# Two decoder layers on one Trainium2 core: loads, the memory branch and the merge's input reordered, a pair's copies ahead of its rests, four tiles normalised on VectorE alone

## The chip, the core and the metric

The kernel runs on one core of one Trainium2 chip. The metric is the device time of one execution in microseconds (us), the median of a few runs; lower is better.

## The reference, cut to what matters

Two layers run over x of 1024 tokens by 1024 features. Each layer projects x once, runs four attention branches of four heads each, weights them with learned gates, multiplies by an output matrix and normalises.

```python
def _layer(x, mem, ...):
    h = x @ w_in
    (c_q, c_kv, k_rope, sb_qkv, fox_qkv, fox_f, mem_q, gate_z, merge_r) = _split_last(h, IN_SPLITS)
    q  = _rms_norm(c_q, q_norm) @ w_qb          # MLA: low-rank queries, keys and values
    kv = _rms_norm(c_kv, kv_norm) @ w_kvb
    y_mla = _causal_softmax_attention(q with rope, k with rope, v_mla)
    y_sb  = _stick_breaking_attention(sq, sk, sv)
    y_fox = _causal_softmax_attention(fq, fk, fv, log_decay=c)
    mk, mv = jnp.split(mem @ w_mem_kv, 2, axis=-1)
    y_mem = _memory_attention(mem_q, mk, mv)    # mem: 256 rows
    merge_g = sigmoid(merge_r @ w_merge_up)
    merged = sum over n of merge_g[n] * ((branches[n] * silu(gate_z[n])) @ w_branch[n])
    return _layer_norm(ALPHA * x + merged @ w_out, ln_g, ln_b)
```

## The kernel before

All matrix products run on TensorE in a float32 form that rounds its operands. To keep float32 accuracy each operand is kept as two tiles, a rounded copy ("h") and the rest ("l" = value minus copy), and each product is three matmuls, h by h, l by h, h by l (`passes`, lines 233 to 239, seen in the trace as L236 to L238). The copy is made by ScalarE out of PSUM and the rest by VectorE from the same PSUM tile and the copy (`split_evac`, L145 and L146, with a scale L148 and L149). A pair of heads is stacked in the 128 rows of one product; `stack_pair` (L282, L283) makes the copy and the rest of rows 0 to 63 in tile opA and of rows 64 to 127 in opB. `v_from_T` (L300, L301), `mla_v` (L903, L904) and the memory keys (L778, L779) do the same for their operands. Weights come in as a stream of 128x512 tiles (`wload`: DMA on SP's queue into "wr", three buffers), and GpSimd splits each (`split_pool`, L154 and L157) into wh and wl, four buffers each.

A layer goes like this. Transposed x (`xT`, 8 column blocks by 2 halves of 512 tokens, each as h and l) stays in SBUF. First come the `pA` products (8 token blocks, lines 619 to 630). Then the branches: fox pair 0 and 1, stick-breaking ("sb") pair 0 and 1, memory ("mem"), MLA. `run` interleaves the attention of one pair with the projections of the next. Before the memory branch, `mem_prep` (757 to 787) loads the 1 MB of transposed mem, splits it, and projects memory keys and values with 8 weight tiles; `cq_norm` (744 to 752) sums squares with eight one-column products; the query projection of memory pair 0 follows. Then `last_gates` projects the last gates; between its halves the input of the merge is split (`split_mr`, `split_y`, lines 1076 to 1078) and the weights `wq` are loaded; then `main` (1085) interleaves the MLA input (`mla_ckvT`, `mla_k`, `mla_v`, ...) with the rest of the gates and the first merge steps. `merge` forms gate times branch product. At a layer's end the output product `po` runs over 8 token tiles twice (left and right 512 columns); after the right one `ln(t)` normalises tile t. Tiles 0 to 5 go VectorE (statistics), ScalarE (L1160), GpSimd (gain, L1161), VectorE (bias, L1163). Tiles 6 and 7, marked `direct`, take four VectorE instructions instead (L1149, L1155). In the first layer `transpose_x` (201 to 209) makes xT of the next layer's first half, woven into the products of tiles 6 and 7.

Instructions stand in each engine's queue in an order that is fixed at compile time. A planner (`schedule_with_timeline_sim=True`) writes it from the program order as priority and from its own estimate of durations; the engines then execute in that order, each waiting where an operand or buffer isn't ready. `after(later, earlier)` adds an edge that only orders two instructions. SBUF tiles of 128x512 float32 come from one pool of 64 ("U").

Of the kernel before, what the change touches and what calls it, by code (L numbers as in the profile page):

```python
# [65 lines left out]
def decoder_trunk(ctx: ExitStack, tc: tile.TileContext, x, x_t, mem_t, positions, w_a, w_s, mla_q_norm, mla_w_qb,  # L66
# [223 lines left out]
    def v_from_T(vT, nblk):  # L290
        v = []
        for b0 in range(0, nblk, 4):
# [4 lines left out]
            for b in range(0, n, 2):  # L297
                t = U("v").rearrange("p (b h c) -> p b h c", b=2, h=2)
                s = ps[:, b * P:(b + 2) * P].rearrange("p (b h c) -> p b h c", b=2, h=2)
                act.copy(t[:, :, :, 0:64], s)  # L300
                dve.tensor_tensor(t[:, :, :, 64:128], s, f(t[:, :, :, 0:64]), ALU.subtract)  # L301
# [274 lines left out]
    nc.sync.dma_start(pos_i, positions.rearrange("o (b p) -> p (o b)", p=P), allow_slow_non_contiguous=True)  # L576
# [29 lines left out]
    for layer in range(DEPTH):  # L606
# [32 lines left out]
        nc.sync.dma_start(fb, fox_forget_bias[layer].partition_broadcast(P))  # L639
# [76 lines left out]
        def evac_mr(ps, half):  # L716
            mr[half] = U("mr", F32)
            act.copy(mr[half], ps)
# [4 lines left out]
        nc.sync.dma_start(gq, mla_q_norm[layer].rearrange("(k p) -> p k", p=P), allow_slow_non_contiguous=True)  # L723
        nc.sync.dma_start(gk, mla_kv_norm[layer].rearrange("(k p) -> p k", p=P), allow_slow_non_contiguous=True)
# [32 lines left out]
        def mem_prep():  # L757
            memT = []
            raws = []
            for k0 in range(0, KT, 2):  # L760
                raw = U("memr", F32).rearrange("p (k c) -> p k c", k=2)
                nc.sync.dma_start(raw, mem_t[k0 * P:(k0 + 2) * P, :].rearrange("(k p) c -> p k c", p=P))
                raws.append(raw)
            for raw in raws:
# [4 lines left out]
            yield  # L769
            for pair in range(2):  # L770
# [5 lines left out]
                for t, r0 in zip(ks, (0, 64)):  # L776
                    lo = 64 - r0
                    act.copy(t[r0:r0 + 64, :], ps[r0:r0 + 64, :MEM])  # L778
# [48 lines left out]
        drain(weave(mem_prep(), cq_norm(), 4))  # L827
        drain(proj(stack_pair(mo[0]["q"], SC64)))
# [63 lines left out]
        def mla_v(half):  # L892
            for b in range(0, 4, 2):
# [108 lines left out]
        def split_y(n, half):  # L1002
            for pair in range(2):
# [6 lines left out]

        def split_mr():
            for half in range(2):
                h, l = U("mrh"), U("mrl")
                split_evac(mr[half], h, l)
                mr[half] = (h, l)
# [251 lines left out]
```

## Time and profile before

| | us |
|---|---|
| median of 3 runs (1605.41 to 1606.14) | 1605.91 |
| the profiled execution | 1603.06 |
| its span, first to last instruction | 1601.3 |
| TensorE (PE) busy | 1562.6 (98%) |
| VectorE (DVE) busy | 1040.0 (65%) |
| GpSimd (POOL) busy | 807.4 (50%) |
| ScalarE (ACT) busy | 740.5 (46%) |
| mean granted TensorE clock | 0.996 of full |

PE is the matmul stream, PEld its weight loads; matmuls overlap, so each is listed longer than the distance to the next. SPq is the queue of DMA issues. An instruction's row in a timeline ends with the idle time of its engine just before it and what ended that time.

### The profile page before, as it was taken

How to read it: one execution, taken by the hardware profiler on the slowest of the kernel's cores; microseconds unless marked ns; L12 is line 12 of the kernel's file. 1: busy time of each engine (PE TensorE's matmuls, PEld its weight loads, DVE VectorE, ACT ScalarE, POOL GpSimd, SP SyncE). 2: the span in 40 equal slices, each digit the busy share in tenths (PEclk: the TensorE clock that was granted, in tenths of full speed). 3: DMA queues.
4: the chain of work that ended last, by engine and by line, in shares of the span. 5: the costliest groups of instructions: out<-in, count | busy, mean ns of one | idle time of the engine just before them, and what ended most of it. 6: DMA issues, size and time to landing. Idle time of an engine off the chain costs nothing. (4 is left out here: it accounts for less than half of the span.)

```text
span 1601.3 us, 24815 instructions
## 1 busy us (share of the span) xinstructions
PE 1562.6 (98%) x8454; PEld 1330.3 (83%) x8454; DVE 1040.0 (65%) x2051; ACT 740.5 (46%) x1632; POOL 807.4 (50%) x967
## 2 busy tenths in 40 slices
PE   9999999999999999999999999999999999999997
PEld 7888888888878788888898888888888778888885
DVE  6365689834436788872763566997344367888737
ACT  4355565534425666440323556565344356564302
POOL 5675535755563233671426665357655623446503
PEclk9999999999999999999999999999999999999998
DMA  5321112142233211252312221122322322212413
GB/s 182 110 60 54 47 43 64 50 119 62 78 121 92 70 37 60 79 172 79 115 61 86 63 59 42 37 71 79 92 60 83 120 83 70 64 43 80 145 53 112
DMA packets 86062, 127.93 MB, mean 80 GB/s; under 512 B 13424, under 2 KB 38832, under 8 KB 85936
## 3 DMA queue, kind: packets, MB, share of 16 engines
q1 hardware_dynamic: 85936, 126.34, 25.5%
q8 instruction: 67, 1.10, 0.3%
q14 instruction: 59, 0.48, 0.1%
HBM read 89.57 MB, written 19.96 MB: 68 GB/s over the span
## 5 line engine op out<-in xcount | busy, mean ns | idle before, releaser
L236 PE MATMUL pj<-xTh,wh 128*128 128x512 f32 x832 | 329.9, 397 | 2.4 <-DVE mx L400 1.4
L238 PE MATMUL pj<-xTh,wl 128*128 128x512 f32 x832 | 326.2, 393 | 0.0
L237 PE MATMUL pj<-xTl,wh 128*128 128x512 f32 x832 | 325.8, 392 | 0.0
L157 POOL TENSOR_TENSOR wl<-wr,wh 128x512 fp32r<-128x512 f32 x168 | 225.7, 1345 | 9.0
L146 DVE TENSOR_TENSOR pl<-pt,ph 128x384 fp32r<-128x384 f32 (+1 forms) x272 | 170.6, 639 | 70.8 <-ACT ph L145 68.1
L154 POOL TENSOR_SCALAR wh<-wr 128x512 fp32r<-128x512 f32 x168 | 115.9, 690 | 198.2 <-PE pj L237 101.1
L145 ACT CAST ph<-pt 128x384 fp32r<-128x384 f32 (+1 forms) x272 | 146.4, 551 | 131.9 <-PE pt L431 128.0
L412 POOL TENSOR_SCALAR p<-p,sm 128x896 f32<-128x896 f32 (+7 forms) x128 | 102.2, 799 | 167.1 <-DVE sm L411 165.1
L238 PEld LDWEIGHTS pj<-xTh,wl 128*128 128x128 f32 x832 | 156.2, 188 | 32.1
L236 PEld LDWEIGHTS pj<-xTh,wh 128*128 128x128 f32 x832 | 156.6, 188 | 29.3 <-DVE mx L400 1.8
L237 PEld LDWEIGHTS pj<-xTl,wh 128*128 128x128 f32 x832 | 156.5, 188 | 26.1
L125 ACT ACTIVATE p<-p,mx 128x896 f32<-128x896 f32 (+7 forms) x128 | 99.5, 777 | 67.1 <-DVE mx L400 60.4
L461 PE MATMUL y<-pl,v 128*128 128x256 f32 (+1 forms) x544 | 121.4, 303 | 0.0
L461 PE MATMUL y<-ph,v 128*128 128x256 f32 (+1 forms) x544 | 111.4, 283 | 1.7 <-ACT ph L145 1.6
L125 ACT ACTIVATE mg<-pg 128x512 f32<-128x512 f32 x128 | 76.4, 597 | 75.0 <-PE pg L238 46.7
L431 PE MATMUL pt<-ident_r,p 128*128 128x128 f32 x704 | 110.7, 273 | 0.0
L236 PE MATMUL pb<-ybh,wh 128*128 128x512 f32 x256 | 103.0, 402 | 3.5 <-ACT mg L125 2.1
L461 PEld LDWEIGHTS y<-ph,v 128*128 128x128 f32 x544 | 93.1, 189 | 14.9 <-ACT ph L145 2.9
L405 DVE TENSOR_TENSOR_SCAN kt<-kt,unseen 128x896 f32<-128x896 f32 (+3 forms) x64 | 97.9, 1542 | 10.0 <-ACT kt L125 9.8
L392 POOL TENSOR_SCALAR_AFFINE_SELECT bt<-bt 128x128 f32<-128x128 f32 x64 | 52.9, 831 | 94.2 <-ACT bt L125 85.3
L237 PE MATMUL pb<-ybl,wh 128*128 128x512 f32 x256 | 100.2, 391 | 0.0
L238 PE MATMUL pb<-ybh,wl 128*128 128x512 f32 x256 | 100.1, 391 | 0.0
(275 smaller groups left out, 3634.6 us busy)
## 6 DMA issues: line engine op xcount, KB each, us to landing
wr<-in_w_s_dram SPq DMA_DIRECT2D x168, 256.0 KB, 2.6
s<-opA SPq DMA_DIRECT2D x128, 64.0 KB, 2.0
s<-opB SPq DMA_DIRECT2D x128, 64.0 KB, 2.0
wr<-in_w_out_dram SPq DMA_DIRECT2D x32, 256.0 KB, 2.7
xr<-in_x_t_dram SPq DMA_DIRECT2D x16, 256.0 KB, 5.7
ckb<-c_d SPq DMA_DIRECT2D x8, 512.0 KB, 3.8
y_d<-y SPq DMA_DIRECT2D x16, 256.0 KB, 2.0
y<-y_d SPq DMA_DIRECT2D x16, 256.0 KB, 3.3
```

Of the source, the lines that this page charges most:

```text
L125: i = act.activation(*args, **kw)
L145: act.copy(h, src)
L146: return dve.tensor_tensor(l, src, f(h), ALU.subtract)
L154: i = pool.tensor_scalar(h, src, 1.0, 1.0, ALU.mult, ALU.mult)
L157: pool.tensor_tensor(l, src, f(h), ALU.subtract)
L236: pe.matmul(ps, ah, bh, start=k == 0, stop=False)
L237: pe.matmul(ps, ah, bl, start=False, stop=False)
L238: pe.matmul(ps, al, bh, start=False, stop=k == nk - 1)
L405: dve.tensor_tensor_scan(kt[:, ::-1], kt[:, ::-1], unseen[:, S - w:][:, ::-1], 1.0, ALU.mult, ALU.max)
L412: pool.tensor_scalar(p, p, sm, 1.0, ALU.mult, ALU.mult)
L431: pe.transpose(pt[:, c:c + P], self.p[i][:, b * P:(b + 1) * P], ident)
L461: pe.matmul(u.y[:, q0 * P:256], u.op["v"][b][:, u.head, :], src[:, s * 256 + q0 * P:s * 256 + 256], start=j == 0 and n == 0, stop=j == n_c ...
```

## The change

Eight edits:

1. The first four weight loads, the positions, the forget bias and the two norm gains are ordered behind the last load of x on SP's queue.
2. `stack_pair`, `v_from_T`, the memory keys and `mla_v` issue both copies of a pair first and then both rests.
3. `merge_r` is split as soon as its product is done (`evac_mr`); `split_mr` goes.
4. Memory: the loads are issued, then the query projection of memory pair 0 runs with the split of mem and `cq_norm` (now in nine steps and more) woven in one step per pass, and the key and value projections come after. The weight stream is reordered to match.
5. The split of the fox branch for the merge is cut in four steps inside `main`, behind `mla_k(0)` and `mla_k(1)`; the load of wq goes to the same place.
6. `ln` takes the direct form from tile 4 on.
7. `transpose_x` of the first half starts after tile 4 and not 5.
8. Its splits take VectorE out: ScalarE copies PSUM to a raw tile, ScalarE copies again for h, GpSimd forms l.

```diff
-    def transpose_x(half, tiles):
+    def transpose_x(half, tiles, apart=False):
...
-            split_evac(ps, h, l)
+            if apart:
+                raw = U("xTr", F32)
+                act.copy(raw, ps)
+                act.copy(h, raw)
+                pool.tensor_tensor(l, raw, f(h), ALU.subtract)
+            else:
+                split_evac(ps, h, l)
...
-        nc.sync.dma_start(raw, w_s[n])
+        i = nc.sync.dma_start(raw, w_s[n])
+        if n < 4:
+            after(i, last_load[0])
...
             for t, r0 in ((a, 0), (b, 64)):
+                act.activation(t[r0:r0 + 64, :], ps[r0:r0 + 64, :], AF.Copy, scale=scale)
+            for t, r0 in ((a, 0), (b, 64)):
                 lo = 64 - r0
-                act.activation(t[r0:r0 + 64, :], ps[r0:r0 + 64, :], AF.Copy, scale=scale)
                 dve.scalar_tensor_tensor(t[lo:lo + 64, :], ps[r0:r0 + 64, :], scale, f(t[r0:r0 + 64, :]),
                                          ALU.mult, ALU.subtract)
...
-        nc.sync.dma_start(raw, x_t[k * P:(k + 1) * P, half * HALF:(half + 1) * HALF])
+        last_load[0] = nc.sync.dma_start(raw, x_t[k * P:(k + 1) * P, half * HALF:(half + 1) * HALF])
...
         def evac_mr(ps, half):
-            mr[half] = U("mr", F32)
-            act.copy(mr[half], ps)
+            h, l = U("mrh"), U("mrl")
+            split_evac(ps, h, l)
+            mr[half] = (h, l)
...
                 pe.matmul(ps[:, 2 * b:2 * b + 1], sq[b // 4][:, (b % 4) * P:(b % 4) * P + P], ones[:, 0:1], start=True, stop=True)
+                yield
...
-        drain(weave(mem_prep(), cq_norm(), 4))
-        drain(proj(stack_pair(mo[0]["q"], SC64)))
+        load_mem()
+        drain(weave(proj(stack_pair(mo[0]["q"], SC64)), chain(split_mem(), cq_norm()), 1))
+        drain(mem_prep())
...
-        split_mr()
-        split_y(2, 0)
-        split_y(2, 1)
-        load_wq()
...
-        main = chain(mla_ckvT(), mla_k(0), mla_k(1), step(lambda: load_cq(1)), mla_v(0), mla_v(1),
+        def split_2(half, pair):
+            return step(lambda: split_y(2, half, [pair]))
+
+        main = chain(mla_ckvT(), mla_k(0), split_2(0, 0), mla_k(1), split_2(0, 1), step(load_wq), step(lambda: load_cq(1)),
+                     split_2(1, 0), split_2(1, 1), mla_v(0), mla_v(1),
...
-            direct = t >= NB - 2
+            direct = t >= 4
...
+                    if t == 4 and not last_layer:
+                        early_x = transpose_x(0, [nat.pop(i) for i in range(4)], True)
                     if t == 5 and not last_layer:
-                        early_x = transpose_x(0, [nat.pop(i) for i in range(4)])
...
+    res += tile_of(w_in, MQ0)
     for c0 in (0, 256, P, 256 + P):
         res += tile_of(w_mem, c0)
-    for pair in range(2):
-        res += tile_of(w_in, MQ0 + pair * P)
+    res += tile_of(w_in, MQ0 + P)
```

## Rows read from the trace of the kernel before

**Rows 1.** The page: the span, and the busy time of each engine with its share of the span and its instructions.

```profile
span 1601.3 us, 24815 instructions
PE 1562.6 (98%) x8454; PEld 1330.3 (83%) x8454; DVE 1040.0 (65%) x2051; ACT 740.5 (46%) x1632; POOL 807.4 (50%) x967
```

**Rows 2.** Stretches of 20 us: stretch, length, busy time (and instructions) of PE, PEld, DVE, ACT and POOL, then the granted clock, the DMA share and GB/s. The first lies in stick-breaking attention of layer 1, the others at the merge's input of layers 1 and 2.

```profile
280.00:300.00 20.00, 18.80 (x106) 15.70 (x106) 18.16 (x19) 9.57 (x22) 15.81 (x14) 1.00 0.19 60
460.00:480.00 20.00, 17.59 (x82) 14.17 (x80) 9.27 (x11) 6.25 (x11) 14.18 (x19) 0.91 0.30 94
1260.00:1280.00 20.00, 17.59 (x90) 14.30 (x90) 11.81 (x15) 9.58 (x17) 16.20 (x21) 1.00 0.31 93
```

**Rows 3.** What PE waited for in the whole span: waiting line, releaser, us in total, times, longest.

```profile
PE pb L236 <- ACT mg L125: 2.1, 3, 0.9
PE mk L237 <- DVE meml L146: 1.1, 4, 0.3
PE pA L238 <- DVE xTl L146: 1.1, 2, 0.9
PE pg L236 <- DVE opB L283: 0.9, 2, 0.5
PE mk L236 <- ACT memh L145: 0.5, 2, 0.3
```

**Rows 4.** The start, timeline of SP's queue and of PE: start, length, engine, line, operation, count. The second SP row is the loads of x's second half; the PE row is the first product that reads a streamed weight tile.

```profile
10.92 1.48 SPq L214 DMA_DIRECT2D wr<-in_w_s_dram  x2
14.44 3.87 SPq L530 DMA_DIRECT2D xr<-in_x_t_dram  x8
...
35.04 0.39 PE L236 MATMUL pj<-xTh,wh 128*128 128x512 f32 x1
```

**Rows 5.** The merge's input: VectorE's timeline in layer 1; PE's timeline from the end of its wait to the next product of the gates, layer 1 and then layer 2; and a stretch of 2 us in layer 1, with the granted clock behind POOL's busy time.

```profile
465.98 2.40 DVE L146 TENSOR_TENSOR mrl<-mr,mrh 128x512 fp32r<-128x512 f32 x2
468.30 3.51 DVE L149 SCALAR_TENSOR_TENSOR ybl<-y,ybh 128x512 fp32r<-128x512 f32 x4
...
472.54 0.73 PE L866 MATMUL ckT<-ident_r,ckv 128*128 128x128 f32 x4 [2.41 <-DVE ckTl L149]
476.45 0.40 PE L236 MATMUL pj<-xTh,wh 128*128 128x512 f32 x1
1268.80 0.66 PE L866 MATMUL ckT<-ident_r,ckv 128*128 128x128 f32 x4 [2.41 <-DVE ckTl L149]
1271.13 0.39 PE L236 MATMUL pj<-xTh,wh 128*128 128x512 f32 x1
...
474.00:476.00 2.00, 2.00 (x8) 1.65 (x7) 0.75 (x1) 0.56 (x1) 1.71 (x4) 0.50 0.67 190
```

**Rows 6.** A pair's copies and rests: ScalarE's wait for VectorE over the whole span; then timelines of VectorE, ScalarE and PE at `mla_k` in layer 1.

```profile
ACT opB L282 <- DVE opA L283: 33.2, 37, 3.6
...
482.32 0.68 DVE L283 SCALAR_TENSOR_TENSOR opA<-pj,opA 64x512 fp32r<-64x512 f32 x1 [5.41 <-ACT opA L282]
483.04 0.59 ACT L282 ACTIVATE opB<-pj 64x512 fp32r<-64x512 f32 x1 [0.75 <-DVE opA L283]
488.58 0.69 DVE L283 SCALAR_TENSOR_TENSOR opB<-pj,opB 64x512 fp32r<-64x512 f32 x1 [0.72 <-ACT opB L282]
490.65 0.69 DVE L283 SCALAR_TENSOR_TENSOR opB<-pj,opB 64x512 fp32r<-64x512 f32 x1 [0.66 <-ACT opB L282]
489.42 0.47 PE L236 MATMUL pg<-mrh,wh 128*128 128x512 f32 x1 [0.46 <-DVE opB L283]
491.29 0.50 PE L236 MATMUL pb<-ybh,wh 128*128 128x512 f32 x1 [0.94 <-ACT mg L125]
```

**Rows 7.** The memory branch: GpSimd's two instructions for a weight tile (groups of the page: count, busy us, mean ns), and two matmuls of PE's timeline with 14 others of the same kind between them.

```profile
L157 POOL TENSOR_TENSOR wl<-wr,wh 128x512 fp32r<-128x512 f32 x168 | 225.7, 1345 | 9.0
L154 POOL TENSOR_SCALAR wh<-wr 128x512 fp32r<-128x512 f32 x168 | 115.9, 690 | 198.2 <-PE pj L237 101.1
...
330.40 0.28 PE L236 MATMUL mv<-memh,wh 128*128 128x256 f32 x1
332.20 0.28 PE L236 MATMUL mk<-memh,wh 128*128 128x256 f32 x1
```

**Rows 8.** The boundary between the layers: VectorE's and PE's timelines.

```profile
792.11 2.99 DVE L1163 TENSOR_TENSOR xo<-xo,lnp 128x512 f32<-128x512 f32 x2 [2.31 <-POOL xo L1161]
801.23 0.40 PE L236 MATMUL pA<-wAh,xTh 128*128 128x292 f32 x1 [1.16 <-DVE xTl L146]
808.05 0.40 PE L237 MATMUL pA<-wAl,xTh 128*128 128x292 f32 x1 [0.39 <-POOL wAl L553]
```

**Rows 9.** The end of layer 2: VectorE's timeline (L1193 takes the product of a tile: tile 4, 5 and 7 here; L1163 at 1587.67 is tile 5's; the last row is the last work of the kernel but for its store), and PE's last matmul.

```profile
1573.77 0.69 DVE L1193 SCALAR_TENSOR_TENSOR res<-xr,po 128x512 f32<-128x512 f32 x1 [0.28 <-DMA out_dram<-xo]
1579.21 0.69 DVE L1193 SCALAR_TENSOR_TENSOR res<-xr,po 128x512 f32<-128x512 f32 x1
1587.67 1.76 DVE L1163 TENSOR_TENSOR xo<-xo,lnp 128x512 f32<-128x512 f32 x1 [0.74 <-POOL xo L1161]
1593.30 0.68 DVE L1193 SCALAR_TENSOR_TENSOR res<-xr,po 128x512 f32<-128x512 f32 x1
1597.01 1.41 DVE L1155 SCALAR_TENSOR_TENSOR xo<-xo,rstd,lnp 128x512 f32<-128x512 f32 x2
...
1589.66 0.39 PE L238 MATMUL po<-woh,mgl 128*128 128x512 f32 x1
```

More of the change, by code (lines that the diff above doesn't have):

```diff
@@ L296, in v_from_T @@
                 pe.transpose(ps[:, b * P:(b + 1) * P], vT[b0 // 4][:, b * P:(b + 1) * P], ident)
-            for b in range(0, n, 2):
-                t = U("v").rearrange("p (b h c) -> p b h c", b=2, h=2)
-                s = ps[:, b * P:(b + 2) * P].rearrange("p (b h c) -> p b h c", b=2, h=2)
+            ts = [(U("v").rearrange("p (b h c) -> p b h c", b=2, h=2),
+                   ps[:, b * P:(b + 2) * P].rearrange("p (b h c) -> p b h c", b=2, h=2)) for b in range(0, n, 2)]
+            for t, s in ts:
                 act.copy(t[:, :, :, 0:64], s)
+            for t, s in ts:
                 dve.tensor_tensor(t[:, :, :, 64:128], s, f(t[:, :, :, 0:64]), ALU.subtract)
@@ L575, in decoder_trunk @@
     pos_i = cp.tile([P, NB], I32, name="pos_i")
-    nc.sync.dma_start(pos_i, positions.rearrange("o (b p) -> p (o b)", p=P), allow_slow_non_contiguous=True)
+    after(nc.sync.dma_start(pos_i, positions.rearrange("o (b p) -> p (o b)", p=P), allow_slow_non_contiguous=True), last_load[0])
     pos_f = cp.tile([P, NB], F32, name="pos_f")
@@ L638, in decoder_trunk @@
         fb = tp.tile([P, 4], F32, tag="fb", name=nm("fb"), bufs=1)
-        nc.sync.dma_start(fb, fox_forget_bias[layer].partition_broadcast(P))
+        after(nc.sync.dma_start(fb, fox_forget_bias[layer].partition_broadcast(P)), last_load[0])
         for h in range(4):
@@ L716, in evac_mr @@
         def evac_mr(ps, half):
-            mr[half] = U("mr", F32)
-            act.copy(mr[half], ps)
+            h, l = U("mrh"), U("mrl")
+            split_evac(ps, h, l)
+            mr[half] = (h, l)
         gq = tp.tile([P, 3], F32, tag="gq", name=nm("gq"), bufs=1)
         gk = tp.tile([P, 2], F32, tag="gk", name=nm("gk"), bufs=1)
-        nc.sync.dma_start(gq, mla_q_norm[layer].rearrange("(k p) -> p k", p=P), allow_slow_non_contiguous=True)
-        nc.sync.dma_start(gk, mla_kv_norm[layer].rearrange("(k p) -> p k", p=P), allow_slow_non_contiguous=True)
+        for g, src in ((gq, mla_q_norm), (gk, mla_kv_norm)):
+            after(nc.sync.dma_start(g, src[layer].rearrange("(k p) -> p k", p=P), allow_slow_non_contiguous=True), last_load[0])
         sq = [None, None]
@@ L755, in decoder_trunk, with load_mem @@
         mo = [{}, {}]
[L757 to L759 removed]
+        memT = []
+        mem_raws = []
+        def load_mem():
             for k0 in range(0, KT, 2):
@@ L762, in mem_prep, with split_mem @@
                 nc.sync.dma_start(raw, mem_t[k0 * P:(k0 + 2) * P, :].rearrange("(k p) c -> p k c", p=P))
-                raws.append(raw)
-            for raw in raws:
+                mem_raws.append(raw)
+        def split_mem():
+            for raw in mem_raws:
                 h, l = U("memh"), U("meml")
@@ L776, in mem_prep @@
                 for t, r0 in zip(ks, (0, 64)):
+                    act.copy(t[r0:r0 + 64, :], ps[r0:r0 + 64, :MEM])
+                for t, r0 in zip(ks, (0, 64)):
                     lo = 64 - r0
-                    act.copy(t[r0:r0 + 64, :], ps[r0:r0 + 64, :MEM])
                     dve.tensor_tensor(t[lo:lo + 64, :], ps[r0:r0 + 64, :MEM], f(t[r0:r0 + 64, :]), ALU.subtract)
@@ L899, in mla_v @@
                                       [(wkv_h[k][:, 256:], wkv_l[k][:, 256:]) for k in range(2)], 2)
-                for i in range(2):
-                    t = U("v").rearrange("p (h c) -> p h c", h=4)
-                    src = ps[:, i * 256:(i + 1) * 256].rearrange("p (h c) -> p h c", h=4)
+                ts = [(U("v").rearrange("p (h c) -> p h c", h=4),
+                       ps[:, i * 256:(i + 1) * 256].rearrange("p (h c) -> p h c", h=4)) for i in range(2)]
+                for t, src in ts:
                     act.copy(t[:, :, 0:64], src)
+                for t, src in ts:
                     dve.tensor_tensor(t[:, :, 64:128], src, f(t[:, :, 0:64]), ALU.subtract)
@@ L1000, in load_y, with split_y @@
                         nc.sync.dma_start(y, y_d[r:r + P, half * HALF:(half + 1) * HALF])
-        def split_y(n, half):
-            for pair in range(2):
+        def split_y(n, half, pairs=range(2)):
+            for pair in pairs:
                 h, l = U("ybh"), U("ybl")
@@ L1009, in decoder_trunk @@
         merged = {}
[L1011 to L1015, printed above, removed]
         def merge(n, first, final, following, also=None):
```

6 lines of the change are left out of this document (4 added, 2 removed).

## The prediction

> **What bounds the kernel now.** I read the page first: of a span of 1601.3 us TensorE is busy 1562.6 us, 98% [rows 1]. No other engine is above 65%. So the kernel is TensorE's stream of matmuls plus 38.7 us in which TensorE has nothing to do, and since the change takes no matmul away, it can only win part of those 38.7 us. The next view is therefore the span in stretches of 20 us, to see where they lie: most stretches are full, and the gaps stand in few places, the largest inside the work being 2.41 us at the merge's input, once in each layer [rows 2]. What ends each gap is in the list of TensorE's waits [rows 3]. Last I read the timelines of the engines around those places, to see what stands in front of the releaser in its queue [rows 4 to 6, 8], and the end, where TensorE is done and VectorE is not [rows 9].
>
> **The start.** Two of the first three weight loads are issued at 10.92 and the loads of x's second half at 14.44 [rows 4]; three small loads stand between too. TensorE later waits 1.1 us, in two pieces, for the rest of a tile of that second half [rows 3]. With x first, its loads are issued some 3.5 us earlier (14.44 - 10.92), more than the wait, so the 1.1 us go. What is late instead is the weights: a tile takes GpSimd 0.69 + 1.345 = 2.04 us [rows 7], and the first product that reads one starts at 35.04, some 17 us after the last load of x is now issued (14.44 + 3.87 = 18.31) [rows 4]. That covers the four tiles (8.1 us). If the cover failed, the price would be one tile, 2.0. Gain taken 1.1, bounds -2.0 and 1.1.
>
> **The memory branch.** TensorE waits 1.1 + 0.5 = 1.6 us over both layers for the split of mem [rows 3]. In the new order the query projection (48 products) stands in front and covers the loads. It no longer stands beside the key and value products, though, and those ask much of GpSimd: 15 steps of their stream take 332.20 - 330.40 = 1.80 us, 0.12 each, so the 96 products of a layer take 11.5 us, while their eight weight tiles cost GpSimd 8 x 2.04 = 16.3 us [rows 7]. Without a head start TensorE would wait 4.8 us per layer. Four buffers hold split weights; two belong to the query projection until it ends, so two tiles, 4.1 us, are ready when the memory products start. That leaves 0.7 us per layer. The upper end is 1.6, the lower 1.6 - 2 x 4.8 = -8.0 should the head start fail; with it 1.6 - 1.4 = 0.2. Other products (the attention left over from stick-breaking) can fill, so I take 0.8. The two new rests of `merge_r` per layer on VectorE fall where TensorE has its projection to run; I cost them at nothing, at most one rest of 1.2 us (2.40 for two, [rows 5]) per layer.
>
> **The merge's input.** VectorE's queue shows two rests of mr (2.40 us) and four of the fox branch (3.51 us) in front of the rests of ckT [rows 5]; TensorE's third transposition of ckT waits 2.41 us for the buffer that these free, in both layers alike. The change takes mr's split out altogether and puts the four others behind `mla_k`, so ckT's rests come first: 4.8 us go. In layer 1 the granted clock stands at 0.50 behind that gap, the 1.2 GHz level, and the same products from the end of the wait to the next gate product take 476.45 - 472.54 = 3.91 us against 1271.13 - 1268.80 = 2.33 us in layer 2 [rows 5]. Without a gap this 1.58 goes too.
>
> The Trainium skill, page "TensorE: Matmul & The Clock Gate", part 1, says that half rate is the default and that activity releases it. By that an equal gap could cost layer 2 its clock in other executions, and the sum would be 1.6 larger; the row shows layer 2 at full clock, and I go by the row.
>
> Behind it comes the chain of pairs of `mla_k`. ScalarE's copy of opB waits for VectorE's rest of opA (0.75 here, 33.2 us in 37 times over the span), so one half takes 490.65 - 488.58 = 2.07 us [rows 6]. The end of that chain holds the first merge product 0.46 us and the second 0.94 us [rows 6]; over both layers 0.9 and some 1.8 of the 2.1 [rows 3], 2.7. With both copies first, ScalarE passes on after two copies (2 x 0.59) and VectorE needs two rests (2 x 0.69 = 1.38 us per half), 0.69 less for each of four halves, 2.8 us: more than the 1.40 that TensorE waits. The four moved rests (3.51 us) now stand among these, so I take 2.0 of 2.7. If they fall on the chain, it is nothing. Term: 4.8 + 1.6 + 2.0 = 8.4, bounds 3.0 (the rests of 3.51 us delay the next wait per layer by about what was won, and the 1.6 and 1.4 stay) and 9.1.
>
> The Trainium skill, page "PSUM — Partial Sum Buffer", section "PSUM bank collisions raise a hardware error", lets two engines use one bank at a time if they are in different groups of 32 partitions. The copy of rows 64 to 127 need not wait for the rest of rows 0 to 63 by that; the row shows that it does. If the page held for the new order, the first rest would not wait for the second copy and all 2.7 would go, sum 0.7 larger.
>
> **The other pairs.** Elsewhere TensorE is mostly full while pairs are evacuated, so I take 0.5. A gain of up to 3 is possible where stick-breaking leaves TensorE idle (1.2 us in one stretch, VectorE busy 18.16 of 20, [rows 2]). The loss: with copies first VectorE's first rest waits for one more copy, 0.59 [rows 6]; in the run of stick-breaking pair 0, near that load, lie four such halves per layer: 8 x 0.59 = 4.7.
>
> **The boundary.** VectorE waits 2.31 us for GpSimd's gain of tile 5, with the rests of the new xT behind it, and TensorE waits 1.16 for such a rest and 0.39 for a weight of pA [rows 8]. Tiles 4 and 5 now ask nothing of GpSimd, VectorE has none of these eight rests, and transposition starts one tile earlier (a tile is 1579.21 - 1573.77 = 5.44 us, [rows 9]). GpSimd gets eight rests of 1.345 us (as its wl, [rows 7]), 10.8 us, instead of four gains, and has two tiles' time, 10.9 us, for it. The cover is thin only at the start: transposition needs tile 3, which still goes the long way, and should TensorE come to it too early it waits what VectorE does now, 2.31. Taken 1.2 of 1.55; bounds -0.8 (1.55 - 2.31) and 1.55.
>
> **The end.** TensorE is done at 1589.66 + 0.39 = 1590.05, VectorE takes tile 7 at 1593.30 and ends at 1597.01 + 1.41 = 1598.42 [rows 9]. So VectorE is 3.25 late, because it waits for GpSimd in each tile (0.74 at 1587.67, [rows 9]). A direct tile costs VectorE 1598.42 - 1593.30 = 5.12, less than a tile of TensorE, 5.44. From tile 4 (1573.77): add the two bias steps of tile 3 (some 1.2) and its wait (some 0.65 as now in the tile before): 1573.77 + 5.12 + 1.85 = 1580.74; three more direct tiles: 1596.1. That is 2.3 earlier. Bounds 0 and 3.23 (1590.07 + 5.12 = 1595.19).
>
> **The sum.** 1.1 + 0.8 + 8.4 + 0.5 + 1.2 + 2.3 = 14.3 us. Against the profiled execution's 1603.06 that is 1588.8. That execution lies 2.85 us under the median of the runs, so against 1605.91 I forecast 1591.6, 0.9% faster. All upper ends together: 1.1 + 1.6 + 9.1 + 3 + 1.55 + 3.23 = 19.6, 1586.3.
>
> **Rivals.**
> - *The stall at the merge moves.* The four rests stand in VectorE's queue in front of the pairs of `mla_k`, and TensorE waits there. For it: the queue's order is planned, and VectorE's 2.31 at the boundary [rows 8] shows a planned order in which one engine stands waiting for another. Against it: VectorE is busy only 9.27 of the 20 us [rows 2]. Price: the 4.8 and the 2.0 are given back, 14.3 - 6.8 = 7.5, time 1598.4. Chance 0.22.
> - *Little of it arrives.* The merge gives nothing (8.4) and the boundary or the memory branch lose 2.3 to 2.8: the gain is at most 3.2, within what a measurement of this kernel can tell from no change, about 0.2%; time about 1603 to 1609, in the middle 1605. For it: every engine's queue is planned anew, and several moved steps share VectorE and GpSimd. Against it: the gaps are shown in both layers alike, and what stood in front of them is gone from the code. Chance 0.09.
> - *Copies first makes it slower.* Place: VectorE's queue in front of each of the 56 pairs of copies and rests (L282, L283: fourteen products of two halves, in two layers). VectorE's first rest waits 0.59 longer, and what stands behind it, the softmax and scan steps, waits too. If each of the 56 were on the path: 33.0, time 1591.6 + 33.0 = 1624.6. It decides from 14.3 / 0.59 = 25 pairs on; slower by over 0.2% needs 17.5 / 0.59 = 30. For it: VectorE is near full in stick-breaking [rows 2]. Against it: only eight of the 56 lie there, and ScalarE loses its own 33.2 us of waiting [rows 6]. Chance 0.06.
>
> **Chances and range.** The forecast 0.63, the stall that moves 0.22, little 0.09, slower 0.06. Faster by over 0.2%: 0.85; within: 0.09; slower: 0.06. The range goes from 1586 (the upper ends) to 1602, which takes in the moved stall with some of the lower bounds and leaves out the last two cases and a little at each edge.
>
> **What would show it.** In the trace after: no wait of ckT's transposition for ckT's rest, and a clock of 1.00 in that stretch; no wait of pA's h by l product in the first 30 us; copies opA and opB back to back on ScalarE; VectorE's last instruction about 6 us after TensorE's and not 8.4; TensorE idle some 25 us instead of 38.7. It is wrong if TensorE's waits for VectorE's L283 or L149 grow at `mla_k`, if GpSimd's wl ends waits of the memory products for more than 0.7 us per layer, or if transposition waits for tile 3.

## The result and the profile after

The changed kernel takes 1594.72 us (median of 4, 1594.06 to 1596.12), the kernel before 1606.02 in the same comparison (1605.41 to 1606.14): ratio 0.9931, 95% interval 0.9919 to 0.9943. It is faster by 0.7%, 11.3 us, where 14.3 were forecast (1591.6, range 1586 to 1602). The profiled execution took 1594.06, its span is 1592.3; against the 1603.06 of before that is 9.0 us. The two differences, 9.0 and 11.3, are not the same thing, and the clock is the likely reason for most of that (below). One execution of e2 (below) took 2027.03 us at a mean granted clock of 0.71; the ratio leaves it out, the median given for e2 counts it.

Line numbers after are larger: `passes` is L245 to L247, `stack_pair` copies at L290 and leaves rests at L293, the direct norm is L1164 and L1170, the long way L1176 (GpSimd) and L1178 (VectorE). The page's first lines, which answer [rows 1]:

```profile
span 1592.3 us, 24853 instructions
PE 1559.3 (98%) x8454; PEld 1328.6 (83%) x8454; DVE 1027.2 (65%) x2047; ACT 737.7 (46%) x1628; POOL 810.3 (51%) x967
```

What TensorE waited for in the whole span (waiting line, releaser, us, times, longest), which answers [rows 3]:

```profile
PE sc L353 <- ACT bt L125: 5.6, 6, 2.0
PE pt L442 <- DVE pl L146: 3.8, 6, 0.9
PE sc L353 <- DVE opB L293: 2.4, 6, 0.6
PE pb L245 <- ACT ybh L148: 2.0, 2, 1.0
PE pb L245 <- DVE opB L293: 1.7, 2, 0.8
...
PE pj L245 <- DVE opB L293: 1.2, 2, 0.6
PE qpT L1006 <- ACT qpe L1008: 1.2, 2, 0.6
```

TensorE has nothing to do for 1592.3 - 1559.3 = 33.0 us; it was 38.7. The waits for ckT's rest [rows 5], for mem, for the xT of x's second half [rows 3] and for a weight of pA [rows 8] are gone. In their place stand waits that the list of before did not have or had smaller: a product of stick-breaking (`sc`) for ScalarE's `bt` 5.6 us, `sc` for a rest of opB 2.4, the first products behind `mla_k` for opB and ybh.

How far each part moves is seen by when TensorE comes to the same product in the two timelines:

| TensorE's product | before | after | moved |
|---|---|---|---|
| first that reads a streamed weight | 35.04 | 32.66 | -2.38 |
| MLA's first score (its part with `kpe`) in layer 1 | 537.71 | 532.80 | -4.91 |
| first output product of layer 1 | 707.29 | 703.83 | -3.46 |
| first that reads a streamed weight in layer 2 | 830.51 | 824.16 | -6.35 |
| MLA's first score (the same part) in layer 2 | 1332.23 | 1324.30 | -7.93 |
| last output product of layer 2 | 1589.66 | 1582.08 | -7.58 |
| (VectorE's last instruction, its end) | 1598.42 | 1589.36 | -9.06 |

Start and boundary gave more than forecast, the two layers' insides far less: some 1.1 us in layer 1 and 1.2 in layer 2 between the weights' first product and the output product.

**The merge's input.** Timelines of PE (its waits only) and of VectorE in layer 1, answering [rows 5, 6]:

```profile
479.45 0.50 PE L245 MATMUL pj<-ckTh,wkvh 128*128 128x512 f32 x1 [0.61 <-DVE opB L293]
483.98 0.47 PE L245 MATMUL pb<-ybh,wh 128*128 128x512 f32 x1 [0.84 <-DVE opB L293]
487.74 0.50 PE L245 MATMUL pb<-ybh,wh 128*128 128x512 f32 x1 [0.97 <-ACT ybh L148]
...
478.00 0.68 DVE L293 SCALAR_TENSOR_TENSOR opA<-pj,opA 64x512 fp32r<-64x512 f32 x1 [6.15 <-ACT opB L290]
478.70 0.69 DVE L293 SCALAR_TENSOR_TENSOR opB<-pj,opB 64x512 fp32r<-64x512 f32 x1
...
481.56 0.83 DVE L149 SCALAR_TENSOR_TENSOR ybl<-y,ybh 128x512 fp32r<-128x512 f32 x1
...
485.29 0.69 DVE L149 SCALAR_TENSOR_TENSOR ybl<-y,ybh 128x512 fp32r<-128x512 f32 x1
```

Two stretches there, with the granted clock behind POOL's busy time, answering [rows 2, 5]:

```profile
474.00:476.00 2.00, 2.00 (x14) 1.63 (x14) 0.00 (x0) 0.53 (x1) 0.00 (x0) 1.00 0.00 0
460.00:480.00 20.00, 19.39 (x100) 15.87 (x99) 5.54 (x8) 7.36 (x13) 5.08 (x5) 1.00 0.15 49
```

The 2.41 us at ckT are gone and the clock stays at full speed. But VectorE, idle for 6.15 us up to 478.00, then works without a pause to 485.98: eight rests of pairs, two rests of the fox branch that were moved here, a gate. TensorE waits three times here, 2.42 us: twice for a rest of opB, the third time for ScalarE's copy of the fox branch (`ybh`).

**The end.** VectorE's, GpSimd's and PE's timelines, answering [rows 9]:

```profile
1568.28 1.77 DVE L1178 TENSOR_TENSOR xo<-xo,lnp 128x512 f32<-128x512 f32 x1 [0.68 <-POOL xo L1176]
1570.93 0.69 DVE L1178 TENSOR_TENSOR xo<-xo,lnp 128x512 f32<-128x512 f32 x1
1587.95 1.41 DVE L1170 SCALAR_TENSOR_TENSOR xo<-xo,rstd,lnp 128x512 f32<-128x512 f32 x2
...
1566.94 2.56 POOL L1176 TENSOR_TENSOR xo<-xo,lnp 128x512 f32<-128x512 f32 x2 [3.17 <-ACT xo L1175]
...
1582.08 0.39 PE L247 MATMUL po<-woh,mgl 128*128 128x512 f32 x1
```

VectorE ends at 1587.95 + 1.41 = 1589.36, 6.9 us after TensorE's 1582.47; it was 8.4.

### The profile page after: what moved, and what is told of

It reads as the page before. It is cut to its first block, busy times and chain, and to the rows that moved or that the text cites. A ratio compares the mean times of both kernels' runs of the same rounds, so it can differ in the third digit from the quotient of the medians.

```text
span 1592.3 us, 24853 instructions
## 1 busy us (share of the span) xinstructions
PE 1559.3 (98%) x8454; PEld 1328.6 (83%) x8454; DVE 1027.2 (65%) x2047; ACT 737.7 (46%) x1628; POOL 810.3 (51%) x967
## 4 chain that ended last, share of the span: by engine, by line
PE 83%; DVE 7%; POOL 3%; issue 3%; ACT 2%; DMA 2%; SPq 0%; DVEq 0%; ACTq 0%; POOLq 0%
PE pj L245 12%; PE pj L246 12%; PE pj L247 12%; PE y L472 6%; PE pt L442 6%; PE sc L353 3%; PE pb L245 3%; PE sc L354 3%; PE pb L246 3%; PE pb L247 3%; PE po L245 3%; PE po L247 3%; PE po L246 3%; PE pg L245 1%; PE pg L247 1%
## 5 line engine op out<-in xcount | busy, mean ns | idle before, releaser
L245 PE MATMUL pj<-xTh,wh 128*128 128x512 f32 x832 | 330.3, 397 | 0.0
L247 PE MATMUL pj<-xTh,wl 128*128 128x512 f32 x832 | 326.6, 392 | 0.0
L154 POOL TENSOR_SCALAR wh<-wr 128x512 fp32r<-128x512 f32 x168 | 121.9, 726 | 212.9 <-PE pj L246 118.1
L247 PEld LDWEIGHTS pj<-xTh,wl 128*128 128x128 f32 x832 | 156.4, 188 | 31.3
L245 PEld LDWEIGHTS pj<-xTh,wh 128*128 128x128 f32 x832 | 156.5, 188 | 26.6 <-DVE mx L411 1.2
L245 PE MATMUL pb<-ybh,wh 128*128 128x512 f32 x256 | 102.8, 402 | 4.7 <-ACT ybh L148 2.0
L247 PE MATMUL pb<-ybh,wl 128*128 128x512 f32 x256 | 100.1, 391 | 0.0
L442 PEld LDWEIGHTS pt<-ident_r,p 128*128 128x128 f32 x704 | 84.7, 140 | 16.1 <-DVE pl L146 2.3
```

Of the source, the lines that this page charges most:

```text
L154: i = pool.tensor_scalar(h, src, 1.0, 1.0, ALU.mult, ALU.mult)
L245: pe.matmul(ps, ah, bh, start=k == 0, stop=False)
L247: pe.matmul(ps, al, bh, start=False, stop=k == nk - 1)
L442: pe.transpose(pt[:, c:c + P], self.p[i][:, b * P:(b + 1) * P], ident)
```

## The experiments

None of these kernels leaves out work. Each is compared with the kernel before on the same chip; ratios with 95% intervals. In the expectations, theories are named as they are told there. The main theory was formed on the trace after: the copies ahead of the rests cost TensorE some 4 us in stick-breaking, and the rest of the change earned more than the total shows. Its rival: the order of copies is neutral, and the gain was lost at the merge.

### Rests between the copies again (e1)

The changed kernel with edit 2 undone in all four places.

```diff
             for t, r0 in ((a, 0), (b, 64)):
-                act.activation(t[r0:r0 + 64, :], ps[r0:r0 + 64, :], AF.Copy, scale=scale)
-            for t, r0 in ((a, 0), (b, 64)):
                 lo = 64 - r0
+                act.activation(t[r0:r0 + 64, :], ps[r0:r0 + 64, :], AF.Copy, scale=scale)
                 dve.scalar_tensor_tensor(t[lo:lo + 64, :], ...)
```

> The changed kernel with edit 2 alone undone: copy, rest, copy, rest in all four places. Theory A: the copies first cost TensorE 2.05 us per layer in fox and stick-breaking attention (its idle time there is 5.88 us in layer 1 against 3.83 before), through the order of VectorE's and ScalarE's queues. Then the 2.01 us wait for bt at the stick-breaking scores goes, and the time falls by 4.1 us, less at most 2.7 that come back at mla_k: 1590.6 to 1593.3. Rival B: those waits come from the whole plan being shifted by the earlier start, and stay: 1594.7 to 1597.4.

Measured: 1590.46, ratio 0.9896 (0.988 to 0.9912); its profiled execution has a span of 1585.2, 7.1 under that of the changed kernel. The place in stick-breaking of layer 1, in the changed kernel, VectorE, ScalarE and PE:

```profile
219.07 4.28 DVE L416 TENSOR_TENSOR_SCAN kt<-kt,unseen 128x896 f32<-128x896 f32 x2
223.28 1.43 DVE L417 TENSOR_TENSOR bt<-bt,kt 128x895 f32<-128x895 f32 x1
...
224.80 1.08 ACT L125 ACTIVATE bt<-sc 128x512 f32<-128x512 f32 x2 [2.25 <-DVE bt L417]
...
225.45 0.39 PE L353 MATMUL sc<-opB,opB 128*128 128x256 f32 x1 [2.01 <-ACT bt L125]
```

and with the rests between the copies:

```profile
216.81 2.10 DVE L414 TENSOR_TENSOR_SCAN kt<-kt,unseen 128x896 f32<-128x896 f32 x1
219.01 1.93 DVE L415 TENSOR_TENSOR bt<-bt,kt 128x895 f32<-128x895 f32 x1
...
223.16 2.28 DVE L414 TENSOR_TENSOR_SCAN kt<-kt,unseen 128x1024 f32<-128x1024 f32 x1
...
220.98 0.60 ACT L125 ACTIVATE bt<-sc 128x512 f32<-128x512 f32 x1 [3.79 <-DVE bt L415]
...
221.63 0.38 PE L351 MATMUL sc<-opB,opB 128*128 128x256 f32 x1 [0.66 <-ACT bt L125]
```

With copies first VectorE has two scans one behind the other (4.28 us) before the subtraction for which ScalarE and then TensorE wait; with the rests between them it has one scan, the subtraction, and the second scan afterwards. The wait is 2.01 instead of 0.66. In fox and stick-breaking together TensorE's waits above 0.2 us are 5.9 us a layer in the changed kernel and 3.9 here, as in the kernel before (3.8). So 2 us a layer, 4.1 in all, come from edit 2. 1.35 of each 2 go through an order of scans that stands behind a pair and is no part of it; the rest is made up of three waits for rests of opB in fox attention and small changes of others. In all, TensorE's idle time is 3.5 us lower than in the changed kernel (29.5) and its busy time 3.6 (1555.7), at full clock in both up to the last products. The busy time is lost in the same place as the waits, as the time between the same two products shows, from the first that reads a streamed weight to ckT's first transposition (fox, stick-breaking and memory):

| kernel | layer 1 | layer 2 |
|---|---|---|
| before | 426.47 | 427.27 |
| changed kernel | 427.72 | 427.79 |
| e1 | 423.88 | 424.59 |
| e7 (below) | 423.81 | 425.29 |

Edit 2 costs 3.84 + 3.20 = 7.0 us here, 4.1 of it as waits above 0.2 us; for the rest the products start a little further apart, for a reason that the traces do not tell. Behind ckT nothing is left between the two: up to the first output product the changed kernel takes 243.45 and 243.32 us, e1 243.41 and 243.33.

The measured time lies just under what theory A allowed (1590.6 to 1593.3), and rival B is out.

### Copies first in MLA alone (e2)

As e1, but the pairs of MLA (`mla_k`, `mla_q`) and `mla_v` keep the copies first.

```diff
-                stack_pair(ml[pair]["k"], 1.0)(ps, half)
+                stack_pair(ml[pair]["k"], 1.0, True)(ps, half)
...
-                stack_pair(ml[pair]["q"], SC96)(ps, half)
+                stack_pair(ml[pair]["q"], SC96, True)(ps, half)
```

> The changed kernel with copies first only in mla_k, mla_q and mla_v, and copy, rest, copy, rest elsewhere. Theory A: stick-breaking as in the run with edit 2 undone, mla_k as in the changed kernel: 1590.6, and by up to 2.7 us faster than with edit 2 undone. Rival B: 1594.7, no change. Rival C, that the order at mla_k does not matter once ckT's rests stand first: equal to the run with edit 2 undone within 0.5 us.

Measured: 1587.70, ratio 0.9887 (0.987 to 0.9905), span 1585.0. That is e1 within its interval (spans 1585.2 and 1585.0); the executions of e1 go from 1586.93 to 1591.57, so the 2.8 us between the two medians decide nothing, and the traces are nearer to rival C. Behind `mla_k` of layer 1 TensorE waits 0.61, 0.84, 0.99, 0.55 and 0.68 here, and 0.65, 0.75, 0.68, 0.97, 0.31, 0.27 and 0.44 in e1: 3.67 against 4.07. At the chain itself the order gives what was forecast: its waits are 2.44 us against 3.36. Later in MLA 0.5 of the 0.9 is lost again, so that a few tenths of a us a layer remain in layer 1, and 0.1 in layer 2.

### The pairs' order alone (e3)

The kernel before with edit 2 alone, as in the diff ahead of the prediction.

```diff
+            for t, r0 in ((a, 0), (b, 64)):
+                act.activation(t[r0:r0 + 64, :], ps[r0:r0 + 64, :], AF.Copy, scale=scale)
             for t, r0 in ((a, 0), (b, 64)):
                 lo = 64 - r0
-                act.activation(t[r0:r0 + 64, :], ps[r0:r0 + 64, :], AF.Copy, scale=scale)
```

> The kernel before with edit 2 alone. Theory A: 4.1 us lost in fox and stick-breaking attention, at most 2.7 won at mla_k (waits of pg and pb): 1606.0 + 1.4 = 1607.4, from 1606 to 1610. Rival B (the order of a pair is harmless, the prediction's 0.5 won): 2.5 to 3.2 us faster, 1603.

Measured: 1616.12, ratio 1.0057 (1.0043 to 1.007): slower by 9.2 us (0.0057 x 1606), far more than theory A had (1606 to 1610), and against rival B. TensorE's waits:

```profile
PE sc L344 <- ACT bt L125: 5.5, 6, 2.0
PE ckT L869 <- DVE ckTl L149: 4.8, 2, 2.4
PE y L463 <- ACT ph L145: 2.5, 2, 1.4
PE sc L344 <- DVE opB L284: 2.4, 6, 0.6
...
PE pb L236 <- DVE opB L284: 1.0, 2, 0.5
```

Two stretches of 4 us, with the granted clock behind POOL's busy time:

```profile
224.00:228.00 4.00, 2.00 (x14) 1.80 (x14) 3.11 (x4) 1.86 (x4) 3.29 (x3) 0.92 0.02 4
1132.00:1136.00 4.00, 3.22 (x15) 3.22 (x16) 2.47 (x7) 3.15 (x5) 0.41 (x1) 0.50 0.17 64
```

The new waits of stick-breaking are the same as in the changed kernel, so they belong to this edit and not to its company. At the first two merge products the order does what the prediction said: they wait for 0.52 us a layer (the line for `pb`), where it was 0.46 + 0.94. Idle time grew by 4.3 us (43.0 against 38.7): 4.4 more in fox and stick-breaking, 2.7 more in the memory branch, 2.2 less at the merge, 0.8 less at the start. The 2.7 have no counterpart in the changed kernel, whose memory branch has no idle time. Most of the rest is clock: behind six of its gaps the granted clock fell to its lower level, 1.2 GHz, for some time, where the profiled execution of before has one such place.

### All tiles normalised on VectorE (e4)

The changed kernel with every tile `direct`.

```diff
-            direct = t >= 4
+            direct = True
```

> The changed kernel with all eight tiles of a layer in the direct form. Theory: at the end VectorE loses what tile 3's bias steps cost beside GpSimd (a wait of 0.68 and 2.3 us), and a direct tile takes it 5.04 us against 5.44 of TensorE, so it ends 5.2 us after TensorE's last product and not 6.9: 1.7 us faster, 1593.0. In layer 1 the transposition finds tile 3 earlier; worth 0 to 0.3. Rival: eight direct tiles in a row let VectorE fall behind TensorE (5.04 is near 5.44, and other work stands beside it), or hold TensorE at layer 1's boundary: 1594.7 or more.

Measured: 1592.78, ratio 0.9914 (0.99 to 0.9928), span 1590.2, 2.1 under the changed kernel. VectorE's last tile:

```profile
1582.20 0.69 DVE L1208 SCALAR_TENSOR_TENSOR res<-xr,po 128x512 f32<-128x512 f32 x1 [0.31 <-PE po L247]
1585.91 1.42 DVE L1170 SCALAR_TENSOR_TENSOR xo<-xo,rstd,lnp 128x512 f32<-128x512 f32 x2
```

VectorE now waits for TensorE at every tile (0.31 at the last) and ends 1587.33 - 1582.16 = 5.2 us behind it, one direct tile. What stood between 5.2 and the 6.9 of the changed kernel is the long way of the tiles before. That is what was expected (1593.0); the intervals of e4 and of the changed kernel overlap, so the 1.7 us rest on the traces.

### Each other part alone, on the kernel before (e5 to e8)

The edits are those of the diff ahead of the prediction: edit 1 (e5), edits 3 and 5 (e6), edit 4 (e7), edits 6 to 8 (e8). One line of each:

```diff
+            after(i, last_load[0])
...
+            split_evac(ps, h, l)
+            mr[half] = (h, l)
...
+        drain(weave(proj(stack_pair(mo[0]["q"], SC64)), chain(split_mem(), cq_norm()), 1))
...
+            direct = t >= 4
```

> The kernel before with edit 1 alone (loads of x first). Theory: the first weight product starts 2.4 us earlier, as in the changed kernel (35.04 to 32.66), of which the prediction counted 1.1: 1606.1 - 2.4 = 1603.7. The rest would be waits of x's first half and of its weights, which the small loads no longer delay. Rival: only the 1.1 are this edit's, the rest another's: 1605.0.

> The kernel before with edits 3 and 5 alone. Theory: the two waits of ckT, 4.8 us, and the slow clock behind them (1.6 in the profiled run) go, the waits behind mla_k stay as they are: 1606.1 - 6.4 = 1599.7, from 1598 to 1601. Rival (the prediction's moved stall): the four rests land on mla_k's pairs and TensorE waits there for what it won: 1604.5 or more.

> The kernel before with edit 4 alone. Theory: the waits for mem's split (1.6 us in both layers) and 0.4 per layer for the first left-over product go: 1606.1 - 2.3 = 1603.8. Rival: GpSimd's weights (16.3 us for 11.5 us of products) make TensorE wait, up to 4.8 per layer: 1606 to 1613.

> The kernel before with edits 6, 7 and 8 alone. Theory: 2.9 at the boundary of the layers (waits 1.16, 0.39 and 0.22 gone and products no longer stretched by the transpositions beside them) and 1.4 at the end: 1606.1 - 4.3 = 1601.8. Rival: the boundary's gain needs the other edits, only the end's 1.4 stays: 1604.7. With the three other single edits the sum should be that of the changed kernel with edit 2 undone, 15.6; if the parts share gains or create new waits together, it is not.

| kernel | median | ratio and interval | gain in us (of 1605.9) |
|---|---|---|---|
| e5, start | 1602.51 | 0.9977 (0.9967 to 0.9986) | 3.7 (2.2 to 5.3) |
| e6, merge's input | 1601.78 | 0.9973 (0.9963 to 0.9982) | 4.3 (2.9 to 5.9) |
| e7, memory | 1599.12 | 0.995 (0.9934 to 0.9967) | 8.0 (5.3 to 10.6) |
| e8, end and boundary | 1601.28 | 0.9971 (0.9958 to 0.9985) | 4.7 (2.4 to 6.7) |
| e3, pairs | 1616.12 | 1.0057 (1.0043 to 1.007) | -9.2 (-11.2 to -6.9) |

The four gains add up to 20.7, with the loss of e3 to 11.5; the whole change has 11.1 by its ratio. So the parts are about additive in sum, and the forecast that was near the total was near it with every large term off. The comparison announced with e8 comes out less well: the four alone give 20.7, while e1, which has all four, gives 16.7 (14.1 to 19.3); and edit 2 costs 9.2 alone but 5.6 in company (by the ratios of e1 and of the changed kernel). The 20.7 are uncertain by some 4 us, so gains that the parts share are neither shown nor ruled out. Of the single forecasts, start (2.4) and end (4.3) lie within the measured intervals; memory (2.3) and the merge's input (6.4) do not. The merge's input gives 4.3 where its term was 8.4, the pairs take 9.2 where +0.5 stood, memory and start give more than their terms.

What e6 does at the merge is seen in its trace. The wait at ckT is gone in both layers; behind `mla_k` TensorE waits, in layer 1:

```profile
485.12 0.50 PE L236 MATMUL pb<-ybh,wh 128*128 128x512 f32 x1 [0.75 <-ACT mg L125]
486.75 0.47 PE L236 MATMUL pg<-mrh,wh 128*128 128x512 f32 x1 [0.67 <-DVE opB L283]
488.66 0.50 PE L236 MATMUL pb<-ybh,wh 128*128 128x512 f32 x1 [0.98 <-ACT ybh L148]
```

With 0.65 at 480.56 and 0.31 at 489.47 that is 3.36 us, and 3.36 in layer 2, against 1.40 of before: 1.96 a layer more, with the order of copies left as it was; the steps of the fox branch's split (`ybh`, `ybl`) now stand among the pairs. The changed kernel, which adds the copies first, has 2.42. So the two effects stand apart: the moved split costs 1.96 a layer here, the order of the copies wins 0.9.

In memory's stretch (300 to 360 in layer 1, 1096 to 1156 in layer 2) the busy time of PE, first of the kernel before, then of e7:

```profile
300.00:360.00 60.00, 58.79 (x356) 51.41 (x355) 30.53 (x47) 26.67 (x57) 37.27 (x37) 1.00 0.33 93
1096.00:1156.00 60.00, 58.56 (x350) 50.74 (x349) 30.26 (x47) 26.32 (x57) 36.63 (x36) 1.00 0.32 93
```

```profile
300.00:360.00 60.00, 60.00 (x367) 53.23 (x366) 32.00 (x50) 28.07 (x61) 40.07 (x41) 1.00 0.32 95
1096.00:1156.00 60.00, 59.73 (x364) 52.91 (x363) 31.99 (x49) 28.07 (x61) 38.98 (x40) 1.00 0.34 99
```

The 1.21 + 1.44 us without work become 0 + 0.27, a gain of 2.4. That is less than the 5.3 at the lower end of what was measured. By the table under e1 the stretch up to ckT is shorter by 2.66 and 1.98, 4.6 us: the products also start closer together. Layer 2 of e7's execution has a piece at half clock in this stretch (from 999.6), which cost it some 1.6 by the estimate of [rows 5]; without it the gain would be some 6, within the interval.

### The version that these point to (e9, e10)

e9 is e2 with every tile direct. e10 also puts two of the four steps of the fox branch's split ahead of the pairs of `mla_k` in program order, meant for the 6 us in which VectorE stood idle.

```diff
-        main = chain(mla_ckvT(), mla_k(0), split_2(0, 0), mla_k(1), split_2(0, 1), step(load_wq), step(lambda: load_cq(1)),
-                     split_2(1, 0), split_2(1, 1), mla_v(0), mla_v(1),
+        main = chain(mla_ckvT(), split_2(0, 0), split_2(0, 1), mla_k(0), split_2(1, 0), mla_k(1), split_2(1, 1), step(load_wq), step(lambda: load_cq(1)),
+                     mla_v(0), mla_v(1),
```

> The changed kernel with copies first only in mla_k, mla_q and mla_v, and with all eight tiles direct: both gains found so far together. Theory (they lie in different stages and add): 1587.7 - 1.9 = 1585.8, VectorE's last instruction 5.2 us behind TensorE's. Rival (the plan changes as a whole and new waits open): 1587 to 1591.

> As the run before, with the four steps of the fox split spread differently in main: two between ckT and mla_k(0), one behind mla_k(0), one behind mla_k(1). Theory: TensorE's wait for ybh at a merge product (0.98 per layer) goes, since the copy is made while ScalarE and VectorE are idle before mla_k; the waits for opB (0.61 and 0.84) stay: 2.0 us faster than the run before, 1583.8. Rival: the rests delay ckT's or kpe's evacuation or mla_k's pairs and the wait of 2.41 of the kernel before comes back in part: 1586 to 1590.

Measured: e9 1585.97, ratio 0.9873 (0.9857 to 0.989); e10 1585.51, ratio 0.9872 (0.9857 to 0.9887). Both are 1.3% under the kernel before and clearly under the changed kernel; between them nothing can be told. e9 came out as its theory said, e10 between its theory and its rival. PE's waits in e10 at the place in question:

```profile
476.05 0.50 PE L245 MATMUL pj<-ckTh,wkvh 128*128 128x512 f32 x1 [1.38 <-DVE gate L814]
481.28 0.47 PE L245 MATMUL pb<-ybh,wh 128*128 128x512 f32 x1 [1.19 <-DVE opB L295]
```

2.57 us here, 0.61 + 0.84 + 0.98 = 2.43 in e9. VectorE and ScalarE just before, in e10:

```profile
474.10 1.29 DVE L149 SCALAR_TENSOR_TENSOR ybl<-y,ybh 128x512 fp32r<-128x512 f32 x2 [5.65 <-ACT ybh L148]
...
472.46 1.07 ACT L898 CAST kpe<-kpT 128x512 fp32r<-128x512 f32 x2 [4.88 <-PE kpT L896]
473.42 1.16 ACT L148 ACTIVATE ybh<-y 128x512 fp32r<-128x512 f32 x2
```

The rests did not come into the idle time. The planner set ScalarE's copies of `ybh` behind its casts of `kpe`, which wait for TensorE, so VectorE is idle for 5.65 us up to 474.10, and the two rests then delay a gate and the pairs by what they saved behind them. So e10 shows that this order moves the wait; whether a plan that uses those 5.65 us would win it was not tested.

### What the clock does to all of them

In each execution of the kernel before in these comparisons, 37 on three chips, the mean granted clock is recorded beside the time:

| mean granted clock | executions | mean time |
|---|---|---|
| 0.992 and 0.993 | 5 | 1607.5 |
| 0.994 | 15 | 1606.8 |
| 0.995 | 14 | 1605.8 |
| 0.996 | 2 | 1604.3 |
| 0.997 | 1 | 1602.9 |

The same gap at ckT, 2.39 to 2.41 us, is in layer 1 and 2 of before, of e5 and of e8. The stretches of 4 us behind it, with the granted clock, of before:

```profile
472.00:476.00 4.00, 3.46 (x13) 2.93 (x14) 1.89 (x3) 1.25 (x2) 3.71 (x8) 0.62 0.46 116
1268.00:1272.00 4.00, 3.20 (x18) 2.76 (x19) 2.80 (x5) 1.38 (x2) 3.81 (x9) 1.00 0.39 92
```

of e5:

```profile
472.00:476.00 4.00, 4.00 (x14) 3.30 (x13) 1.50 (x2) 0.80 (x2) 3.63 (x6) 0.57 0.64 187
1268.00:1272.00 4.00, 4.00 (x16) 3.20 (x15) 1.50 (x2) 1.37 (x2) 3.69 (x7) 0.65 0.73 192
```

and of e8, which loses clock at memory (324) and not at ckT in layer 1:

```profile
324.00:328.00 4.00, 4.00 (x21) 4.00 (x22) 2.52 (x7) 2.45 (x4) 1.22 (x2) 0.59 0.10 37
472.00:476.00 4.00, 4.00 (x22) 3.40 (x23) 1.99 (x3) 1.38 (x2) 3.54 (x8) 1.00 0.49 139
```

So a gap of 2.4 us, or the row of small waits at memory, is followed by half clock in some executions and in others not, and once costs some 1.6 us ([rows 5]: 3.91 against 2.33). A gap that is removed is worth its own length and a share of 1.6. The profiled executions of the changed kernel, e1, e2, e4, e9 and e10 have no stretch under full clock before TensorE's last products, and the times of e9 and e10 lie close together (1585.08 to 1586.75, at a mean clock of 0.998 and 0.999 in all eight; the kernel before in the same comparison: 1605.13 to 1608.14, at 0.994 and 0.995).

## Why the prediction was right, and where its steps failed

The sign, the range and the place of most gains held. That the total lies so near the forecast is luck: by the last column below, merge, pairs and end fell short by 12.6 us, and memory, boundary and start made good 7.5 of them. The terms in the profiled executions, by waits and clock, and by the time between the same products (memory from e1 against before, the pairs from the changed kernel against e1, as in the table under e1):

| term | forecast | by waits and clock | between the same products |
|---|---|---|---|
| start | 1.1 | 2.4 | 2.4 |
| memory | 0.8 | 2.4 | 5.3 |
| merge's input | 8.4 | 4.5 | 4.1 |
| other pairs | +0.5 | -4.1 | -7.0 |
| boundary | 1.2 | 2.9 | 2.9 |
| end | 2.3 | 1.5 | 1.5 |
| sum | 14.3 | 9.6 | 9.2 (9.0 measured) |

**Start.** Right in kind: the waits for the xT of x's second half are gone and the weights are early enough. Mis-sized, because only the 1.1 for xT was counted; waits of the first products for their split weights (0.56 and 0.26 at 10.5 and 11.6 in the trace of before) went too, and the first weight's product moved by 2.38 (with edit 1 alone, e5, it starts at 32.54).

**Memory.** GpSimd's head start held: no wait over 0.2 us for wl stands here in the trace after, and one of 0.27 in that of e7. The term was too small on three counts. It took off 0.7 us a layer for GpSimd's weights, which did not come. It took the list's two lines for mem alone and left out two waits of 0.39 for `ph` in memory attention, which the new order covers as well. And it counted waits only, while the products here also start closer together.

**The merge's input** is the term that failed as the first rival said. The wait at ckT went (4.8), the dip of the clock in layer 1 went (1.6). But waits of 0.61, 0.84, 0.97, 0.58 and 0.68 us stand behind it in layer 1 against 0.46, 0.94, 0.24, 0.65 and 0.29 before. Over both layers waits here fall by 3.0 us, not by 6.8; with the clock 4.5. The chain of the pairs was costed rightly: with the copies first the waits at its end fall from 1.40 to 0.52 us a layer (e3 against before) and from 3.36 to 2.42 (the changed kernel against e6), and ScalarE's waits for the rests vanished (33.2 us in [rows 6], not in the list any more). The step that failed is "The four moved rests (3.51 us) now stand among these, so I take 2.0 of 2.7": it set aside 0.7 us for them over both layers, and with them there, and the old order of copies, these waits are 1.96 a layer longer (e6). The rival gave back the whole 6.8; in the trace it took 3.8 of them. The prediction named the right queue and was wrong in the argument against it: VectorE's 9.27 busy us of 20 [rows 2] is a mean over a stretch in which its work comes in one piece, 8 us without a pause behind 6 us of idling in the changed kernel.

**The other pairs** had the wrong sign. The bound of -4.7 covers the waits (-4.1) but not the time between the products (-7.0), nor the loss of edit 2 alone (-9.2, from -11.2 to -6.9). The third rival had the direction but not the form: no pair loses 0.59 as such. What costs is a new order in VectorE's queue, two scans in a row where one stood, a wait of 2.01 instead of 0.66, and three new waits in each layer for rests of opB (2.4 us over both). The planner writes all queues anew, and here it placed much of the loss where no edit is.

**Boundary and end.** At the boundary all of the 1.55 and a wait of 0.22 went; transposition did not wait for tile 3. The other 1.1 us are no wait that the trace lists: the same products start closer together there (e8 alone: 2.75 us between the first output product and layer 2's first streamed weight). At the end the step "two bias steps of tile 3 (some 1.2)" was mis-sized: they take 1.77 + 0.69 = 2.46, since the first runs beside GpSimd's second gain. Without tiles on the long way (e4) the end is 5.2 behind TensorE, the value in the prediction's upper bound.

**What it said would show it.** Right: no ckT wait, clock 1.00 behind it, no h by l wait in the first 30 us, copies back to back, no wait for tile 3. VectorE ends 6.9 behind, where 6 was said. Wrong: 33.0 us of idle TensorE instead of some 25. And one of its signs of being wrong came up: the waits for the pairs' rests (L283 of before, L293 after) at `mla_k` grew from 0.46 to 0.61 + 0.84 us in layer 1. It was the sign of the step that failed.

**The profiled execution and the median.** The sum was set against the median with an offset of 2.85 us taken to stay. It did not: the changed kernel's profiled execution lies 0.66 under its median. Judged by the table of clocks, the 2.85 were mostly clock lost behind gaps in other executions (the clock of those three executions is not known), and the largest gaps went. The sentence with the Trainium skill's page "TensorE: Matmul & The Clock Gate", part 1, that an equal gap may cost layer 2 its clock in other executions was the better reading: e5 shows 0.65 in that stretch. Deciding for the one row of layer 2 left out a gain of up to 1.6 us in such executions; how much of it is in the median is not shown.

The page "PSUM — Partial Sum Buffer" of the Trainium skill, section "PSUM bank collisions raise a hardware error", would let the first rest start beside the second copy. Here it starts at 478.00, when the copy of opB (477.37, 0.59 long) is done. That is a wait that stands in the program as built; it tells nothing of whether the chip needs it.

## What to carry to other kernels

Cost a stall together with the work that will stand there afterwards: read the engine's queue for the next 10 us, not its mean share of a stretch, and look in the trace after whether a step that was moved in the program also moved in time. Here 6 us in which VectorE idled stayed unused, and the wait only changed its place. Where a planner orders the queues, test each part alone and each part undone: here one of five parts cost 9 us alone while the whole was faster by 11, and leaving it out of the whole was worth some 6 to 7, more than any other refinement. A gap in TensorE's stream was worth its own length here and, in some executions, some 1.6 us of clock on top, so compare several executions before a single profile decides about one or two us.

## What was not expected of the hardware

One and the same gap is followed by half clock in one execution or layer and not in another: 2.4 us at ckT were followed by a granted clock of 0.62 and 1.00 (before, layers 1 and 2), 0.57 and 0.65 (e5) and 1.00 (e8, layer 1). The mean time of the kernel before goes from 1602.9 to 1607.5 as the mean clock falls from 0.997 to 0.992 and 0.993.

A bias step on VectorE (two SBUF inputs, 128x512) takes 1.77 us while GpSimd works on its next gain (1566.94 to 1569.50 for the two) and 0.69 alone. The Trainium skill, page "SBUF — State Buffer", section "Who interferes with whom", says that a VectorE instruction with two SBUF inputs contends with a GpSimd instruction that reads SBUF. The trace agrees: the step ends at 1570.05, 0.55 us after the 1569.50 at which GpSimd ends, about the length it has alone.
